# A hybrid encoder layer on one core: the shared sums queued later, two small product groups on column halves, the last norm's parameters loaded later

## The chip, the cores and the metric

The kernel runs on one core of a Trainium2 chip. The core has TensorE (PE, matrix products into PSUM), VectorE (DVE), ScalarE (ACT), GpSimd (POOL) and SyncE (SP), whose queue issues most DMAs here. Each engine runs its own instructions in order, and semaphores tie them together. The metric is the device time of one execution in microseconds (us); lower is better.

## The reference, cut to what matters

One layer of width 1024 over 1024 tokens, with 16 learned tokens put in front and dropped at the end, all in float32. The stream is projected once; three mixers read the projection (HGRN2 heads, Mamba-2 heads, S5 channel groups); their outputs are concatenated and projected, and a squared-ReLU MLP of width 4096 follows.

```python
proj = h @ w_in[l]
q_a, f_a, i_a, g_a, z_b, xbc_b, dt_b, u_c = jnp.split(proj, split_idx, axis=-1)
y_a = hgrn2_mixer(q_a, f_a, i_a, g_a, ...)   # 6 heads, chunks, a decay per channel
y_b = mamba2_mixer(z_b, xbc_b, dt_b, ...)    # 6 heads, chunked state space
y_c = s5_mixer(u_c, ...)                     # diagonal complex recurrence
mixed = jnp.concatenate([y_a, y_b, y_c], axis=-1) @ w_out[l]
h = layer_norm(ALPHA * h + mixed, ln1_g[l], ln1_b[l])
ff = jnp.square(jax.nn.relu(h @ w_mlp_in[l])) @ w_mlp_out[l]
h = layer_norm(ALPHA * h + ff, ln2_g[l], ln2_b[l])
```

In the HGRN2 mixer, a chunk's output is what the state before it gives, plus the products of q and k within the chunk, each pair of tokens weighted by the decay between them.

## The kernel before

**Precision.** A large product is made of float32 halves: `split` (L98) casts a tile to a high part on ScalarE (L100) and subtracts it on VectorE for the low part (L87), and `mm3` (L107) adds three products, high by high, high by low and low by high (L108 to L110).

**Weights.** `load_raw` (L182) issues on SP the DMA of a 128x512 half tile into one of a ring of four raw buffers; the split puts it into one of eight pairs of high and low tiles. A load therefore waits until the split of four loads before is done, and a split until the products are done that last read its pair. In the last phase a second ring of four joins.

**Order of the work.** The program is written as lists of small steps (units), and `run` (L1578) merges several lists in proportion. The framework then builds each engine's own instruction order from this program order as priority, by its own estimate of when things are ready, and fixes it: on the chip an engine never passes an instruction that waits. What order two instructions of one engine get can be forced with an ordering edge between them.

**The mixers.** HGRN2 works on 8 chunks of 128 tokens, 4 in each half of the sequence. Within a chunk, `hg_level` (L777) goes through seven levels h = 1, 2, 4 to 64: at each, products of the running `A` (decayed q) and `B` (decayed k) give the scores between the neighbouring blocks of length h. At levels up to 32 there is one product for each of three channel tiles and each half of the tokens (L791), the halves going to PSUM partitions 0 to 63 and 64 to 127, that is to the array's two column halves. The last level (L783) has one product a channel tile for both heads of it, with its output on partitions 0 to 63 alone, and ScalarE copies it to `Py` (L785). `hg_out` (L805) first forms the sums of q times k per token (L810): `QK` as weights with all 128 columns, against a constant with two columns, for each channel tile; then the other products of the chunk's output in 64-column halves (L814 to L817).

**Output projection.** `wout_units` (L1091) makes, for four token tiles t of a half and two column halves dh, a unit of 24 matmuls and one accumulation into `acc[t]` on VectorE (`accumulate`, L1079). The first unit of a dh loads the eight w_out half tiles, for dh = 0 also the eight mixed tiles. PSUM for it comes from a ring of two (`p_o`).

**MLP.** The 4096 hidden columns are done in 8 pieces of 4 tiles of 128. Pieces 0 to 3 run plainly over the first half of the tokens, piece 0 then over the second half (`p0`: four upward units "u", one weight fetch "w", eight downward units "d"). Pieces 4 to 7 run over both halves with a seven-product Strassen scheme upward (`up_strassen`, L1290) and downward (`strassen_units`, L1390 on). Pieces 1 and 2 over the second half form one more Strassen block, the double piece, and piece 3 over the second half ends the kernel.

**Shared sums.** The four Strassen pieces share sums of the normed input, made once by `row_sums` (L1246): `fetch3` and `third` subtract two halves of the first tokens' rows (they need only the first half of the tokens), `first`, `second` and `fourth` need the second half too. All but `second` write their split result to DRAM (`away`, T_d), from where `stream(n)` (L1239) brings sum n into the tiles of the first half's input, four DMAs of 512 KB, before each piece that needs it. In a piece, `w5` loads four w_mi half tiles, adds two pairs (`tw`) on VectorE and splits them for the first product, on sum 1.

**Where the change touches.** The eight units of `fetch3` and `third` are merged with the eight units of the second half's output projection; the sums with p0 by a string of letters ("s" is `stream(1)`); `load_gb(2)` puts scale and shift of the last norm (broadcast to 128 partitions) on SP just ahead of the double piece; `finish(t)` norms and stores the first half's tokens and is merged with the double piece's 32 units.

```python
run(wout_units(1, (6, 7, 0, 1, 2, 3, 4, 5), True), sums[0])
...
for c in "u u f u w f u f f d d s n d n d n d n d d d".split():
    (p0 if c in "udw" else sums[1]).pop(0)()
...
gb = gbp.tile([128, 2, D], F32, tag="gb", name="gb2")
load_gb(2)
...
run(us, [lambda t=t: finish(t) for t in h0])
```

Of the kernel before, what the change touches and what calls it, by code (L numbers as in the profile page):

```python
# [11 lines left out]
ALU = mybir.AluOpType  # L12
# [8 lines left out]
NPRE = 4  # L21
# [3 lines left out]
ALPHA = 2.0 ** 0.25  # L25
# [41 lines left out]
def tile_trunk(ctx, tc, xT, x_tok, w_vdt, w_ch, w_out, w_mi, w_mo, glu_w, pack, kconst,  # L67
# [15 lines left out]
    def add(e, out, a, b):  # L83
        e.tensor_tensor(out=out, in0=a, in1=b, op=ALU.add)  # L84

# [3 lines left out]
    def stt(out, a, s, b, op0, op1):  # L89
        V.scalar_tensor_tensor(out=out, in0=a, scalar=s, in1=b, op0=op0, op1=op1)  # L90

# [90 lines left out]
    def load_raw(src):  # L182
        rings.append(rings.pop(0))
        raw = rings[-1]()
        nc.sync.dma_start(out=raw, in_=src)
        return raw

    def load_h(src, dst=None):
# [588 lines left out]
    def hg_level(c, h):  # L777
        hb = HB[c % len(HB)]
        ps = p_sc()
        if h == 64:  # L780

            for ct in range(3):
                PE.matmul(ps[0:64, ct * 128:ct * 128 + 128].rearrange("p (g l) -> p g l", g=2),  # L783
                          hb["B"][:, ct, 0:64], hb["A"][:, ct, :, 64:128], start=True, stop=True, skip_group_check=True)
            S.copy(hb["Py"][0:64], ps[0:64, 0:384].rearrange("p (h l) -> p h l", h=6))  # L785
        else:

            for ct in range(3):
                for x in range(2):
                    Av = hb["A"][:, ct, :, hms[x]].rearrange("p g (b two l) -> p g b two l", two=2, l=h)[:, :, :, 1, :]  # L790
                    PE.matmul(ps[hms[x], ct * 64:ct * 64 + 64].rearrange("p (g b l) -> p g b l", g=2, l=h),  # L791
                              hb["B"][:, ct, hms[x]], Av, start=True, stop=True, skip_group_check=True)
            src = ps[:, 0:192].rearrange("p (h b l) -> p h b l", h=6, l=h)
            dst = hb["P"].rearrange("p h (b two l) -> p h b two l", two=2, l=h)[:, :, :, 1, :]
            if h == 32:

                S.copy(hb["Py"][64:128], hb["P"][64:128])
                S.copy(dst[0:32, :, 0], src[0:32, :, 0])
                S.copy(hb["Py"][64:96, :, 32:64], src[64:96, :, 0])
            else:  # L800
                m = km2[:, h.bit_length() - 1].unsqueeze(1).to_broadcast([128, 6, 32])
                V.copy_predicated(dst, m.rearrange("p h (b l) -> p h b l", l=h), src)
        hg_decay(hb, h, 128, True)

    def hg_out(c):  # L805
# [3 lines left out]
        for ct in range(3):  # L809
            PE.matmul(po[:, 384 + 2 * ct:386 + 2 * ct], hb["QK"][:, ct], ind2, start=(ct == 0), stop=False,  # L810
                      skip_group_check=True)
        for h in range(6):
# [261 lines left out]
    def mix_in(half, k):  # L1074
        src_d, o = ((mixA_d, 0), (mixB_d, 3), (mixC_d, 6))[k // 3]
        raw = load_raw(src_d[:, k - o, HALF * half:HALF * half + HALF])
        split(hk(half, 0, POS[k]), hk(half, 1, POS[k]), raw)

    def accumulate(t, dh, lhs, w, first, c0=0, nc_=512):  # L1079

# [5 lines left out]
        if first:  # L1086
            stt(acc[t][:, cs], acc[t][:, cs], ALPHA, ps, ALU.mult, ALU.add)
        else:
            add(V, acc[t][:, cs], acc[t][:, cs], ps)

# [155 lines left out]
    def row_sums(t2h, t2l, pool):  # L1246
# [38 lines left out]
        def units(f):  # L1285
            return [lambda k=k: f(k) for k in range(4)]

        return units(fetch3) + units(third), units(first) + [lambda: stream(1)] + units(second), units(fourth)

    def up_strassen(js, A, t2, again, ahead, beside):  # L1290

# [86 lines left out]

        us += [w5] + go("c", "s1", "1", True, keep(1, 0)) + [lambda: stream(3)] + beside[:2]
        us += [w1] + go("a", "11", "11", True, keep(0, 1)) + beside[2:]  # L1380
# [8 lines left out]

    def strassen_units(fs, ts_, keep, b_op, sums=None, again=False, beside=()):  # L1390

# [162 lines left out]
        if sums is not None:  # L1554
            us += up_strassen(js, A, sums, again, ahead, list(beside))
        else:
# [110 lines left out]
    sums = row_sums(t2h, t2l, ff2)  # L1667
    run(wout_units(1, (6, 7, 0, 1, 2, 3, 4, 5), True), sums[0])
    run(sum([[lambda t=t: norm1(t), lambda t=t: h1_transpose(t)] for t in h1_], []), pre[cut:])
# [3 lines left out]
    p0 = piece(0, [1], (), HALF, True)  # L1673
    for c in "u u f u w f u f f d d s n d n d n d n d d d".split():
        (p0 if c in "udw" else sums[1]).pop(0)()
    for p in range(NPRE, NP):
        js = list(range(NF * p, NF * p + NF))
        for f in strassen_units((js[:2], js[2:]), (list(h0), list(h1_)), True, lambda name: [None] * 2, (t2h, t2l), p < NP - 1,
                                sums[2] if p == NPRE else ()):
            f()  # L1680
    gb = gbp.tile([128, 2, D], F32, tag="gb", name="gb2")
    load_gb(2)
    rings_t2 = lambda: arp.tile([128, 512], F32, tag="t2h", name="raw", bufs=4)
# [5 lines left out]
                        lambda name: [[x[:, j] for x in b4] for j in range(4)] if name in ("b1", "b3", "b7") else [None] * 4)  # L1689
    run(us, [lambda t=t: finish(t) for t in h0])  # L1690
    rings[:] = [f for f in rings if f is not rings_t2]
# [99 lines left out]
```

## Time and profile before

| | |
|---|---|
| median of 3 runs | 1224.56 us (1223.6 to 1226.91) |
| the profiled execution's own time | 1227.8 us |
| its span, first to last instruction | 1225.7 us |
| mean granted TensorE clock | 0.994 of full speed |
| busy: PE, DVE, ACT, POOL | 1194.5, 898.6, 596.0, 24.5 us |
| DMA | 180.97 MB, mean 148 GB/s |

Times in the views count from the span's start. A row of a timeline has the start, the duration, engine, line, operation, the tiles (written <- read), the partitions x elements, a count, and in brackets how long the engine had stood idle before it and what ended that. A row of the view of waits has who waited <- for whom: microseconds in total, times, the longest. A row of the windows view has the stretch, its length, the busy time of the engine with the number of instructions that touch the stretch, the granted clock of TensorE, the busy share of the DMA engines and their GB/s. A row of a group has busy time, mean ns of one, and the idle time before. SPq is SP's queue issuing DMAs; PE records are two for each float32 product that is not split, one for each of a split one.

### The profile page before, as it was taken

The numbers are of one execution on the slowest core, as the hardware profiler recorded it, in microseconds if no ns is written. First come the engines' busy times: TensorE is split into PE (matmuls) and PEld (weight loads), VectorE is DVE, ScalarE is ACT, GpSimd is POOL, SyncE is SP. The second block draws the span as 40 slices with busy tenths as digits, with TensorE's granted clock in tenths as the row PEclk, the third lists the DMA queues.
The fourth block names the chain that finished last, engine by engine and source line by source line (L and its number), as shares of the span: only waits on it lengthen the run. The fifth ranks groups of instructions, "written<-read, shape, count | busy, mean of one in ns | idle before, by whom it ended". The sixth has DMA issues, their size and how long they took to land.

```text
span 1225.7 us, 19167 instructions
## 1 busy us (share of the span) xinstructions
PE 1194.5 (97%) x6932; PEld 984.8 (80%) x6932; DVE 898.6 (73%) x1953; ACT 596.0 (49%) x1312; POOL 24.5 (2%) x35
## 2 busy tenths in 40 slices
PE   8999999999999999999998998999999999999997
PEld 8988788778787888887886886878878778788886
DVE  7824866787777797757564776779597796899956
ACT  5343233544775376545453354463553635546542
POOL 0000000000000000000000000000000000003003
PEclk9999999999999999999998999999999999999999
DMA  8142343224557252323159367863635627357331
GB/s 272 55 148 86 78 122 114 104 85 131 164 187 233 65 151 81 100 79 113 52 170 324 100 180 235 266 198 103 237 106 188 224 71 252 124 160 243 121 112 68
DMA packets 111693, 180.97 MB, mean 148 GB/s; under 512 B 10992, under 2 KB 45424, under 8 KB 111600
## 3 DMA queue, kind: packets, MB, share of 16 engines
q1 hardware_dynamic: 108144, 173.47, 44.5%
q10 hardware_dynamic: 3456, 6.29, 1.3%
q8 instruction: 54, 0.88, 0.3%
q14 instruction: 39, 0.32, 0.1%
HBM read 148.43 MB, written 30.24 MB: 146 GB/s over the span
## 4 chain that ended last, share of the span: by engine, by line
PE 70%; DMA 13%; DVE 11%; ACT 3%; issue 2%; SPq 1%; ACTq 0%; POOL 0%; POOLq 0%; DVEq 0%
PE pg L108 11%; PE pg L109 11%; PE pg L110 11%; PE pm_o L108 7%; PE pm_o L109 7%; PE pm_o L110 7%; DMA raw<-w_mi 4%; PE pm_sc L109 2%; PE pm_sc L110 2%; PE pm_sc L108 2%; PE pm_sc L791 2%; DMA raw<-w_out 2%; DVE lo L87 1%; DMA xr<-xT 1%; DMA raw<-w_mo 1%
## 5 line engine op out<-in xcount | busy, mean ns | idle before, releaser
L87 DVE TENSOR_TENSOR lo<-raw,hi 128x512 fp32r<-128x512 f32 x260 | 177.1, 692 | 120.4 <-ACT hi L100 117.3
L100 ACT CAST hi<-raw 128x512 fp32r<-128x512 f32 x260 | 159.1, 619 | 181.7 <-PE pg L109 79.5
L108 PE MATMUL pm_o<-hi,fh 128*128 128x512 f32 x232 | 94.0, 405 | 3.6 <-DVE acc L90 3.3
L110 PE MATMUL pm_o<-hi,fl 128*128 128x512 f32 x232 | 91.6, 395 | 0.0
L109 PE MATMUL pm_o<-lo,fh 128*128 128x512 f32 x232 | 91.6, 395 | 0.0
L108 PE MATMUL pg<-x0h,hi 128*128 128x264 f32 (+1 forms) x264 | 85.3, 323 | 0.4 <-ACT uch L640 0.4
L108 PE MATMUL pg<-h1a,hi 128*128 128x512 f32 (+1 forms) x224 | 82.7, 370 | 2.2 <-ACT hi L100 1.4
L110 PE MATMUL pg<-x0h,lo 128*128 128x264 f32 (+1 forms) x264 | 84.5, 320 | 0.1
L109 PE MATMUL pg<-x0l,hi 128*128 128x264 f32 (+1 forms) x264 | 83.9, 318 | 0.0
L109 PE MATMUL pg<-h1a,hi 128*128 128x512 f32 (+1 forms) x224 | 81.2, 363 | 0.7 <-DMA h1a<-T_d 0.7
L110 PE MATMUL pg<-h1a,lo 128*128 128x512 f32 (+1 forms) x224 | 81.4, 364 | 0.0
L110 PE MATMUL pg<-h1b,lo 128*128 128x512 f32 x176 | 68.6, 390 | 0.1
L108 PE MATMUL pg<-h1b,hi 128*128 128x512 f32 x176 | 68.5, 389 | 0.0
L109 PE MATMUL pg<-h1b,hi 128*128 128x512 f32 x176 | 68.5, 389 | 0.0
L109 PE MATMUL pg<-x1l,hi 128*128 128x512 f32 x168 | 66.4, 395 | 0.0
L110 PE MATMUL pg<-x1h,lo 128*128 128x512 f32 x168 | 66.3, 395 | 0.0
L108 PE MATMUL pg<-x1h,hi 128*128 128x512 f32 x168 | 66.2, 394 | 0.0
L84 DVE TENSOR_TENSOR acc<-acc,pm_o 128x512 f32<-128x512 f32 (+1 forms) x77 | 52.0, 675 | 18.6 <-PE pm_o L110 17.6
L100 ACT CAST fh<-ar 128x512 fp32r<-128x512 f32 (+1 forms) x72 | 39.5, 560 | 40.5 <-DVE ar L87 32.0
L100 ACT CAST hi<-tw 128x512 fp32r<-128x512 f32 x52 | 31.9, 620 | 51.4 <-DVE tw L87 28.9
L108 PEld LDWEIGHTS pm_o<-hi,fh 128*128 128x128 f32 x232 | 44.1, 190 | 13.4 <-DVE acc L90 3.8
L108 PEld LDWEIGHTS pg<-x0h,hi 128*128 128x128 f32 x264 | 49.6, 188 | 5.2 <-ACT uch L640 0.8
(459 smaller groups left out, 3042.7 us busy)
## 6 DMA issues: line engine op xcount, KB each, us to landing
raw<-w_mo SPq DMA_DIRECT2D x140, 256.0 KB, 3.4
raw<-w_mi SPq DMA_DIRECT2D x112, 256.0 KB, 3.3
h1a<-T_d SPq DMA_DIRECT2D x48, 512.0 KB, 6.4
raw<-w_ch SPq DMA_DIRECT2D x48, 256.0 KB, 3.3
raw<-w_out SPq DMA_DIRECT2D x32, 256.0 KB, 3.8
acc<-x_tok SPq DMA_DIRECT2D x8, 512.0 KB, 5.5
b_d<-sig SPq DMA_DIRECT2D x16, 256.0 KB, 3.0
ar<-b_d SPq DMA_DIRECT2D x16, 256.0 KB, 5.3
```

Source lines behind the costliest of these rows:

```text
L84: e.tensor_tensor(out=out, in0=a, in1=b, op=ALU.add)
L87: e.tensor_tensor(out=out, in0=a, in1=b, op=ALU.subtract)
L100: S.copy(hi, src)
L108: PE.matmul(out, wh, xh, start=start, stop=False, **kw)
L109: PE.matmul(out, wh, xl, start=False, stop=False, **kw)
L110: PE.matmul(out, wl, xh, start=False, stop=stop, **kw)
L791: PE.matmul(ps[hms[x], ct * 64:ct * 64 + 64].rearrange("p (g b l) -> p g b l", g=2, l=h), hb["B"][:, ct, hms[x]], Av, start=True, stop=Tru ...
```

## The change

- The units `fetch3` are now traced after the first five units of the second half's output projection, and their fetches get an ordering edge on SP behind the last w_out load so far (`fetched`). Each `third` gets an edge on VectorE behind the accumulation two before the last one traced (`behind`).
- The last level's product is split by head, one to each column half, 64 moving columns each, and the copy to `Py` becomes two. The sums of q times k are split into the two halves of the tokens, with 64 columns of weights each.
- `stream(1)` is taken out of p0's string; in the first Strassen piece it comes after `w5`, and `w5`'s VectorE instructions get an edge behind the fourth accumulation from the end, the fifth of p0's eight.
- `load_gb(2)` becomes a unit (`last_gb`) merged with the double piece, ahead of the four `finish`, with an edge on SP behind the last load traced before it. With five units merged into 32, it is traced after the seventh, and the `finish` units after the 13th, 20th, 26th and 32nd instead of the 8th, 16th, 24th and 32nd.

```diff
     def load_raw(src):
         rings.append(rings.pop(0))
         raw = rings[-1]()
-        nc.sync.dma_start(out=raw, in_=src)
+        fetched[0] = nc.sync.dma_start(out=raw, in_=src)
         return raw
...
             for ct in range(3):
-                PE.matmul(ps[0:64, ct * 128:ct * 128 + 128].rearrange("p (g l) -> p g l", g=2),
-                          hb["B"][:, ct, 0:64], hb["A"][:, ct, :, 64:128], start=True, stop=True, skip_group_check=True)
-            S.copy(hb["Py"][0:64], ps[0:64, 0:384].rearrange("p (h l) -> p h l", h=6))
+                for g in range(2):
+                    PE.matmul(ps[hms[g], ct * 64:ct * 64 + 64], hb["B"][:, ct, 0:64], hb["A"][:, ct, g, 64:128],
+                              start=True, stop=True, skip_group_check=True)
+            Pg = hb["Py"].rearrange("p (c g) l -> p c g l", g=2)
+            for g in range(2):
+                S.copy(Pg[0:64, :, g], ps[hms[g], 0:192].rearrange("p (c l) -> p c l", c=3))
...
         for ct in range(3):
-            PE.matmul(po[:, 384 + 2 * ct:386 + 2 * ct], hb["QK"][:, ct], ind2, start=(ct == 0), stop=False,
-                      skip_group_check=True)
+            for x in hms:
+                PE.matmul(po[x, 384 + 2 * ct:386 + 2 * ct], hb["QK"][:, ct, x], ind2, start=(ct == 0), stop=False,
+                          skip_group_check=True)
...
+    sums_done = []
+
+    def behind(f, n):
+
+        with tc.issue_after(sums_done[-1 - n].ins):
+            f()
+
     def accumulate(t, dh, lhs, w, first, c0=0, nc_=512):
...
         if first:
-            stt(acc[t][:, cs], acc[t][:, cs], ALPHA, ps, ALU.mult, ALU.add)
+            sums_done.append(stt(acc[t][:, cs], acc[t][:, cs], ALPHA, ps, ALU.mult, ALU.add))
         else:
-            add(V, acc[t][:, cs], acc[t][:, cs], ps)
+            sums_done.append(add(V, acc[t][:, cs], acc[t][:, cs], ps))
...
-        return units(fetch3) + units(third), units(first) + [lambda: stream(1)] + units(second), units(fourth)
+        return units(fetch3) + units(third), units(first) + units(second), units(fourth)
...
-        us += [w5] + go("c", "s1", "1", True, keep(1, 0)) + [lambda: stream(3)] + beside[:2]
+        if first:
+            us += [lambda: behind(w5, 3), lambda: stream(1)]
+        else:
+            us.append(w5)
+        us += go("c", "s1", "1", True, keep(1, 0)) + [lambda: stream(3)] + beside[:2]
...
-    run(wout_units(1, (6, 7, 0, 1, 2, 3, 4, 5), True), sums[0])
+
+    wu = wout_units(1, (6, 7, 0, 1, 2, 3, 4, 5), True)
+    for f in wu[:5]:
+        f()
+    for f in sums[0][:4]:
+        with tc.issue_after(fetched[0].ins):
+            f()
+    for i in range(4):
+        if wu[5 + i:]:
+            wu[5 + i]()
+        behind(sums[0][4 + i], 2)
...
-    for c in "u u f u w f u f f d d s n d n d n d n d d d".split():
+    for c in "u u f u w f u f f d d n d n d n d n d d d".split():
         (p0 if c in "udw" else sums[1]).pop(0)()
...
-    load_gb(2)
+
+    def last_gb():
+
+        with tc.issue_after(fetched[0].ins):
+            load_gb(2)
+
...
-    run(us, [lambda t=t: finish(t) for t in h0])
+    run(us, [last_gb] + [lambda t=t: finish(t) for t in h0])
```

`tc.issue_after(i)` adds the edge to those instructions of its block that run on `i`'s own engine; the block's instructions on other engines get none.

More of the change, by code (lines that the diff above doesn't have):

```diff
@@ L83, in add @@
     def add(e, out, a, b):
-        e.tensor_tensor(out=out, in0=a, in1=b, op=ALU.add)
+        return e.tensor_tensor(out=out, in0=a, in1=b, op=ALU.add)
     def sub(e, out, a, b):
@@ L89, in stt @@
     def stt(out, a, s, b, op0, op1):
-        V.scalar_tensor_tensor(out=out, in0=a, scalar=s, in1=b, op0=op0, op1=op1)
+        return V.scalar_tensor_tensor(out=out, in0=a, scalar=s, in1=b, op0=op0, op1=op1)
     def ts(e, out, a, s1, s2=None, op0=ALU.mult, op1=None):
@@ L184, in load_raw @@
         raw = rings[-1]()
-        nc.sync.dma_start(out=raw, in_=src)
+        fetched[0] = nc.sync.dma_start(out=raw, in_=src)
         return raw
+    fetched = [None]
     def load_h(src, dst=None):
@@ L1286, in units, with up_strassen @@
             return [lambda k=k: f(k) for k in range(4)]
-        return units(fetch3) + units(third), units(first) + [lambda: stream(1)] + units(second), units(fourth)
-    def up_strassen(js, A, t2, again, ahead, beside):
+        return units(fetch3) + units(third), units(first) + units(second), units(fourth)
+    def up_strassen(js, A, t2, first, again, ahead, beside):
         us = []
@@ L1388, in up_strassen, with strassen_units @@
         return us
-    def strassen_units(fs, ts_, keep, b_op, sums=None, again=False, beside=()):
+    def strassen_units(fs, ts_, keep, b_op, sums=None, first=False, again=False, beside=()):
         us = []
@@ L1554, in strassen_units @@
         if sums is not None:
-            us += up_strassen(js, A, sums, again, ahead, list(beside))
+            us += up_strassen(js, A, sums, first, again, ahead, list(beside))
         else:
@@ L1677, in tile_trunk @@
         js = list(range(NF * p, NF * p + NF))
-        for f in strassen_units((js[:2], js[2:]), (list(h0), list(h1_)), True, lambda name: [None] * 2, (t2h, t2l), p < NP - 1,
+        for f in strassen_units((js[:2], js[2:]), (list(h0), list(h1_)), True, lambda name: [None] * 2, (t2h, t2l), p == NPRE, p < NP - 1,
                                 sums[2] if p == NPRE else ()):
```

## The prediction

> **What bounds the kernel now.** The page comes first: which engine fills the span.
>
> ```profile
> span 1225.7 us, 19167 instructions
> PE 1194.5 (97%) x6932; PEld 984.8 (80%) x6932; DVE 898.6 (73%) x1953; ACT 596.0 (49%) x1312; POOL 24.5 (2%) x35
> ```
>
> TensorE is busy 1194.5 of 1225.7 us. What is to be gained is therefore of two kinds: the 31 us in which it stands still, and matmuls that cost fewer of its own microseconds. The view of waits, for PE alone, says who ended its longest pauses (total, times, longest).
>
> ```profile
> PE pm_o L109 <- DVE lo L87: 4.7, 2, 4.1
> PE pm_o L108 <- DVE acc L90: 3.3, 1, 3.3
> PE pg L108 <- ACT hi L100: 1.4, 2, 1.1
> PE pg L109 <- DMA h1a<-T_d: 0.7, 1, 0.7
> PE pg L108 <- DMA h1a<-T_d: 0.7, 1, 0.7
> ```
>
> Two pauses are of over 3 us, and the diff has an edit beside each of these lines. So next the timelines of PE, DVE and SP's queue around the first one.
>
> ```profile
> 656.77 0.50 PE L108 MATMUL pm_o<-hi,h1b 128*128 128x512 f32 x1
> 661.42 0.80 PE L109 MATMUL pm_o<-lo,h1b 128*128 128x512 f32 x1 [4.15 <-DVE lo L87]
> ...
> 660.07 0.69 DVE L87 TENSOR_TENSOR ar<-ar 128x512 f32<-128x512 f32 x1 [4.61 <-DMA ar<-b_d]
> 660.68 0.68 DVE L87 TENSOR_TENSOR lo<-raw,hi 128x512 fp32r<-128x512 f32 x1
> ...
> 652.08 1.83 SPq L1257 DMA_DIRECT2D ar<-b_d  x2
> 656.09 0.84 SPq L1257 DMA_DIRECT2D ar<-b_d  x2
> ...
> 656.10 0.62 ACT L100 CAST hi<-raw 128x512 fp32r<-128x512 f32 x1 [1.11 <-DMA raw<-w_out]
> ```
>
> The reader is to see an order on VectorE, not a lack of speed. TensorE needs the low part of the last w_out half tile (`lo`). The split that makes it stands on VectorE behind a subtraction of the shared sums (`third`), and that one waits 4.61 us for its operand, whose fetch SP issued only at 652 to 656. The windows view shows what follows a pause.
>
> ```profile
> 646.70:656.70 10.00, 10.00 (x46) 1.00 0.93 296
> 661.42:667.57 6.15, 6.15 (x15) 0.50 0.97 317
> 762.76:766.74 3.98, 3.98 (x10) 0.57 0.39 132
> ```
>
> The column after the count is the granted clock: 1.00 before, 0.50 after the pause. 15 matmuls took 6.15 us where at 46 in 10.00 us they would take 3.3, so 2.9 us more went. After the second pause 10 matmuls took 3.98 instead of 2.2 us: 1.8 us more.
>
> **The change part by part.** Terms are against the profiled execution's own 1227.8 us (its span is 1225.7); the median of the runs is 1224.56, 3.2 us lower, and I take that off at the end.
>
> **A, the shared sums.** The eight fetches now stand in SP's queue behind the last w_out half tile, and the four `third` steps on VectorE behind the fourth, fifth and sixth accumulation. Nothing is left between the low part at 660.68 and its cast. Gone are the pause of 4.15 and the slow stretch of 2.9: 7.1 us. What is late next is the w_out half itself: TensorE reached it at 656.77, when its high part had just been cast (656.10 and 0.62), and the low part takes 0.68 more, so I leave 0.4 us of pause: 6.7 gained. Where the sums go, w_out's second halves are loading.
>
> ```profile
> 678.05 2.37 SPq L185 DMA_DIRECT2D raw<-w_out  x4
> ...
> 670.55 0.69 DVE L90 SCALAR_TENSOR_TENSOR acc<-acc,pm_o 128x512 f32<-128x512 f32 x1 [5.20 <-PE pm_o L110]
> ```
>
> VectorE idles 5.20 us per accumulation there, and a `third` needs two subtractions of 0.69, so the work itself is covered. The four late w_out halves are not roomy, which makes a rival below. Queued behind the moved fetches on SP are the next w_mo and w_mi loads; those are fetched ahead of their use.
>
> **B, the first `w5`.**
>
> ```profile
> 762.76 0.50 PE L108 MATMUL pm_o<-hi,fh 128*128 128x512 f32 x1 [3.33 <-DVE acc L90]
> ...
> 761.42 0.69 DVE L84 TENSOR_TENSOR tw<-raw 128x512 f32<-128x512 f32 x1 [5.18 <-DMA raw<-w_mi]
> 762.03 0.68 DVE L90 SCALAR_TENSOR_TENSOR acc<-acc,pm_o 128x512 f32<-128x512 f32 x1
> ...
> 754.34 0.87 SPq L1244 DMA_DIRECT2D h1a<-T_d  x2
> 755.27 7.67 SPq L185 DMA_DIRECT2D raw<-w_mi  x4
> ```
>
> The same pattern: the sum `tw` of the first Strassen piece waits 5.18 us on VectorE for w_mi, and an accumulation that frees a PSUM bank waits behind it. The w_mi loads were late because `stream(1)` stood ahead of them on SP. The change sets `w5`'s VectorE work behind the fifth of eight accumulations and `stream(1)` behind the loads. Gained: 3.33 and 1.8, 5.1 us. `w5` then has three downward products to finish in, 36 matmuls or some 8 us at the rate above, and needs two adds, two casts and two subtractions, some 3 us: covered. But TensorE now comes to this piece 5 us sooner, while its weight loads go through four raw buffers, whose pace is that of DMA.
>
> ```profile
> 775.88 6.64 SPq L185 DMA_DIRECT2D raw<-w_mi  x4
> 784.54 1.85 SPq L1244 DMA_DIRECT2D h1a<-T_d  x4
> ...
> 802.03 2.15 SPq L1244 DMA_DIRECT2D h1a<-T_d  x4
> ```
>
> The streams at 784.54 and 802.03 stand behind such loads, and the second one already gave the pauses of 0.7 and 0.7. If nothing of this queue moves, all 5.1 come back; if it moves with TensorE, nothing does, and if the earlier first stream also helps the later ones, those 1.4 go too. Part of it follows TensorE, since splits wait for tiles that products free, so I charge 1.5 us.
>
> **C, scale and shift of the last norm.**
>
> ```profile
> 1047.40 0.50 PE L108 MATMUL pg<-h1a,hi 128*128 128x512 f32 x1 [1.13 <-ACT hi L100]
> ...
> 1033.84 0.42 SPq L1137 DMA_DIRECT2D gb<-ln_gb  x1
> 1036.58 2.23 SPq L185 DMA_DIRECT2D raw<-w_mi  x2
> ```
>
> One of the two broadcasts is issued ahead of the w_mi loads on which this pause of 1.13 hangs. Moved behind the double piece's fetches it frees them: 1.1 us. In exchange the four norms of the first half come later on an engine that has no room to spare:
>
> ```profile
> 1150.00:1160.00 10.00, 9.99 (x20) 1.00 0.34 109
> ...
> L1112 DVE BATCH_NORM_STATS2 bst<-acc 128x6 f32<-128x512 f32 x8 | 5.2, 665 | 0.0
> L90 DVE SCALAR_TENSOR_TENSOR acc<-acc,mv,gb 128x768 f32<-128x768 f32 x4 | 4.2, 1053 | 0.0
> L90 DVE SCALAR_TENSOR_TENSOR acc<-acc,lrs,gb 128x768 f32<-128x768 f32 x4 | 4.0, 1008 | 0.0
> ```
>
> Only 8.2 us of these norms read gb, and TensorE never waits in that stretch, so I charge nothing; the rival has the other end.
>
> **D, column halves.** Windows of PE that run from a group's first matmul to the start of the next group, and one of mixed half-column matmuls.
>
> ```profile
> 246.42:246.92 0.50, 0.50 (x14) 1.00 0.00 0
> 253.40:254.20 0.80, 0.80 (x8) 1.00 0.57 190
> 612.53:613.19 0.66, 0.66 (x8) 1.00 0.00 0
> 255.26:256.55 1.29, 1.29 (x50) 1.00 0.00 0
> L785 ACT COPY Py<-pm_sc x8: 472/473/477, 254.3 to 609.5; 64x384 f32<-64x384 f32 x8
> ```
>
> The last level now costs 0.80 us a chunk (6 records on one column half); the other levels do the same volume in 12 records on both halves in 0.50. Eight chunks by 0.30: 2.4 us. The sums of q times k take 0.66 (6 full-width records of two columns). As 12 half-width ones at the pace of the fourth row (50 in 1.29, or 0.026 each) they take 0.31, a gain of 0.35 a chunk, or 2.8 in all; at the first row's 0.50 it is 1.3. I take 2.0. No row shows half-width weights with two moving columns, so zero gain is the lower bound; twice the instructions on the same full-width pace would lose 5.3, and the fourth row, where each record has weights of its own, excludes that. The copy of 0.473 becomes two shorter ones on ScalarE, busy 49%: nothing, or at most some 0.2 a chunk if the next product waited for it.
>
> The fourth row is also where a rule of the Trainium skill is to be weighed. "TensorE: Matmul & The Clock Gate", Part 3, says that a weight load overlaps running matmuls only when its row group differs, and column halves share their rows; with its load time of columns over 1.2 GHz, halving the columns and doubling the loads would gain nothing, and the total would be 2.0 us higher. This trace disagrees: 0.026 us per record is less than the 0.053 that the page's formula gives for 64 columns.
>
> **Sum.** 6.7 + 5.1 − 1.5 + 1.1 + 2.4 + 2.0 = 15.8; 1227.8 − 15.8 = 1212.0 on the profiled execution's scale, less 3.2: 1208.8 us.
>
> **The rivals.** *The first Strassen piece gives its gain back.* For it: the two streams above, and a queue that does not reorder. Against it: `stream(1)` no longer blocks the loads, so the queue starts sooner. Price: the rest of B, 3.6, to 1212.4, and up to 1.8 more for a halved clock: about 1214.
>
> *The sums still come in between.* The new order binds one engine each: `third` may start right after the fourth accumulation, just when w_out's last four half tiles (issued at 678.05) are to be split. If a subtraction that waits for its fetch is put ahead of one of those splits, the pause moves to the fifth accumulation. Price: half of A to all of it, 3.4 to 6.7: 1212.2 to 1215.5. This is also the way in which the change would not do what it says.
>
> *Half-width q times k gains nothing.* Then D has 2.4 alone: 1210.8.
>
> *Slower: the norms fall into the full stretch.* If gb lands so late that VectorE has nothing else to do until then, the norms' 5.2 + 4.2 + 4.0 = 13.4 us fall behind the products' splits and accumulations between 1140 and 1170, and TensorE waits for them, with 2.9 us of half clock after each of two pauses: 19.2 us, so 1228.0. It decides from the point at which VectorE, waiting for gb before 1130, idles longer than it is ahead of TensorE; how far ahead that is no row tells, only that the view of waits lists no long pause there. Against it: there are other splits to fill the time with, and the norms need gb for 8.2 of the 13.4 only.
>
> **How the numbers follow.** Forecast 0.62; the first piece gives back 0.17; sums in between 0.10; q times k gains nothing 0.07; slower by the norms 0.04. The lower end: A with 7.1, B with 5.1 and 1.4 of the later stream, C 1.1, D 2.4 + 2.8 make 19.9, so 1204.7; 1204. The upper end takes the rivals up to 1215.5 and 1.5 for a build order that shifts elsewhere: 1217. About 0.3%, or 3.7 us, is what a measurement tells from no change: all cases but the last lie beyond it, and I leave 0.03 for several rivals together: faster 0.93, same 0.03, slower 0.04.
>
> **What would show it.** In the changed kernel PE's waits have no line of 4.1 us on `lo` and none of 3.3 on `acc`; the granted clock is 1.00 after the first output projection unit of the second half; the last level and q times k have twice their matmul records, a group of the first takes 0.50 and one of the second about 0.4; gb is issued after the double piece's first w_mi loads and 1.13 is gone. The first rival shows as PE waits on `h1a<-T_d` of over 3 us in the first Strassen piece, the second as a wait on `lo` at the fifth accumulation, the slower one as waits on `acc` or `fl` near 1140 to 1170. I am wrong if TensorE's pauses sum to more than 20 us.

## The result, and the profile after

The changed kernel took 1217.68 us in the median of six runs (1214.67 to 1220.67), the kernel before 1226.56 in as many beside it (1223.6 to 1228.36): a ratio of the means of 0.9932, 95% interval 0.9914 to 0.9950, or 8.3 us less (6.1 to 10.5). Timed once more in another job, the ratio was 0.9917 (0.9898 to 0.9937), 10.2 us less. The direction was forecast; the size was to be 15.8, to 1208.8 us, and 1217.7 lies just above the forecast's upper end of 1217.

The page of the changed kernel, its first two lines of numbers:

```profile
span 1212.6 us, 19370 instructions
PE 1186.5 (98%) x7028; PEld 976.8 (81%) x7028; DVE 898.2 (74%) x1953; ACT 596.3 (49%) x1320; POOL 24.7 (2%) x35
```

The 96 added matmuls are there, and TensorE is busy 8.0 us less; it stands still for 26.1 us instead of 31.2. The span is 13.1 us shorter, more than the runs are apart, so this pair of executions flatters the change. The profiled execution of the changed kernel (1214.67 us) was the fastest of its six runs, and the one of the kernel before (1227.8) was above its median. The view of waits for PE, between 640 and 830 us, answers to the two long pauses:

```profile
PE pg L108 <- ACT ar L1383: 2.0, 1, 2.0
PE pm_o L108 <- DVE acc L90: 0.8, 1, 0.8
PE pm_o L109 <- DVE lo L87: 0.2, 1, 0.2
```

The pauses of 4.15 on `lo` and 3.33 on `acc` are gone. The first line is new: a product waits for ScalarE's copy of a sum (L1383). The windows view, PE alone: the last level, q times k (both, as in the prediction, from a group's first matmul to the start of the next group), the second output projection, and the stretch after the new pause.

```profile
605.04:605.54 0.50, 0.50 (x14) 1.00 0.00 0
608.80:609.17 0.37, 0.37 (x13) 1.00 0.00 0
646.00:656.00 10.00, 10.00 (x46) 1.00 0.44 138
781.64:787.00 5.36, 5.36 (x16) 0.68 0.33 114
```

The last level takes 0.50 us a chunk as forecast and the sums of q times k 0.37 (0.66 before; about 0.4 forecast). After the new pause the granted clock is 0.68. Where that pause is made, the timelines of SP's queue, ScalarE and PE show:

```profile
765.99 1.54 SPq L185 DMA_DIRECT2D raw<-w_mi  x2
767.58 3.70 SPq L1257 DMA_DIRECT2D h1a<-T_d  x4
772.83 2.13 SPq L185 DMA_DIRECT2D raw<-w_mi  x2
...
774.26 0.59 ACT L1383 COPY ar<-pg 128x512 f32<-128x512 f32 x1
780.48 0.62 ACT L100 CAST hi<-raw 128x512 fp32r<-128x512 f32 x1 [5.63 <-DMA raw<-w_mi]
781.00 0.58 ACT L1383 COPY ar<-pg 128x512 f32<-128x512 f32 x1
...
781.64 0.50 PE L108 MATMUL pg<-h1a,hi 128*128 128x512 f32 x1 [1.97 <-ACT ar L1383]
```

Read it from the bottom. The fourth product of the first Strassen piece adds to a bank whose content must first be copied out. The copy stands on ScalarE behind a cast that waits 5.63 us for w_mi, and that load, issued at 772.83, landed 7.6 us later, behind the four stream fetches of 512 KB each.

To see where gains come and go, take stretches of each profiled execution: from the first matmul of the second output projection to p0 (the sums' pause lies there), from p0 to the first Strassen piece (the pause of `w5`), from the first to the seventh product of that piece, and from its first product to the end of its seventh and last. Starts are those of PE's timeline; all in us. The runs named are told in the next section.

| kernel | projection to p0 | p0 to the piece | first to seventh product | whole piece |
|---|---|---|---|---|
| before | 76.33 | 49.76 | 32.64 | 39.97 |
| before, profiled again | 76.24 | 49.27 | 32.64 | 39.35 |
| changed | 71.37 | 43.83 | 36.56 | 41.99 |
| changed, profiled again | 71.89 | 43.77 | 36.34 | 42.19 |
| sums alone | 71.69 | 48.81 | 32.64 | 38.64 |
| `w5` alone | 74.95 | 43.55 | 36.67 | 42.49 |
| gb alone | 71.25 | 49.89 | 32.66 | 38.86 |
| halves alone | 70.71 | 51.05 | 32.89 | 40.56 |
| sums and `w5` | 71.73 | 43.72 | 38.73 | 45.83 |
| sums and `w5`, no fourth stores | 70.59 | 43.91 | 35.16 | 41.03 |
| changed, no fourth stores | 73.30 | 44.74 | 33.30 | 39.15 |
| changed, fourth sums later | 71.64 | 44.12 | 37.83 | 43.77 |
| changed, weights ahead of sums | 69.74 | 44.61 | 35.42 | 41.27 |
| all but `w5` | 72.24 | 51.06 | 32.64 | 39.01 |

The second and the last column are steady. Over all twenty profiles the second stretch is 43.5 to 45.5 us where `w5` is moved and 48.8 to 51.5 where it is not. The whole piece takes 38.1 to 40.6 us without the move, and 41.2 to 45.8 with it where the stores are made as before. The third column overstates the loss: a part of it comes back in the seventh product, where the kernel before has its two pauses of 0.7 us. The first column is not steady: gb alone and the halves alone keep the old order of the sums, and their stretches are no longer than the changed kernel's.

### The profile page after: what moved, and what is told of

Same layout as the page of the kernel before. It is cut to its first block, busy times and chain, and to the rows that moved or that the text cites. A ratio compares the mean times of both kernels' runs of the same rounds, so it can differ in the third digit from the quotient of the medians.

```text
span 1212.6 us, 19370 instructions
## 1 busy us (share of the span) xinstructions
PE 1186.5 (98%) x7028; PEld 976.8 (81%) x7028; DVE 898.2 (74%) x1953; ACT 596.3 (49%) x1320; POOL 24.7 (2%) x35
## 4 chain that ended last, share of the span: by engine, by line
PE 72%; DVE 12%; DMA 10%; ACT 3%; issue 2%; SPq 0%; POOL 0%; POOLq 0%; DVEq 0%; ACTq 0%
PE pg L108 12%; PE pg L109 12%; PE pg L110 12%; PE pm_o L108 6%; PE pm_o L110 6%; PE pm_o L109 6%; DMA raw<-w_mi 4%; PE pm_sc L109 2%; PE pm_sc L110 2%; PE pm_sc L108 2%; PE pm_sc L796 2%; DVE lo L87 2%; DMA xr<-xT 1%; ACT hi L100 1%; DVE ctg L81 1%
## 5 line engine op out<-in xcount | busy, mean ns | idle before, releaser
L110 PEld LDWEIGHTS pg<-x0h,lo 128*128 128x128 f32 x264 | 49.7, 188 | 3.8 <-issue 0.6
```

The lines of the kernel that those rows point to most:

```text
L110: PE.matmul(out, wl, xh, start=False, stop=stop, **kw)
```

## The experiments

**Theory 1**: the four parts do what the diff says, and part of what they gain is lost again in the first Strassen piece, whose transfers cannot be had sooner, and at the weights behind the moved sums. **Rivals**: the parts never gained that much and the profile of before was of a slow execution; or the new waits come from the order on ScalarE, not from the transfers.

**Each part alone.** The edit of each is its own part of the diff put into the kernel before: the sums' units, `w5` and `stream(1)`, `last_gb`, the two groups of half-width matmuls.

```diff
+    for f in sums[0][:4]:
+        with tc.issue_after(fetched[0].ins):
+            f()
...
+        behind(sums[0][4 + i], 2)
```
```diff
+            us += [lambda: behind(w5, 3), lambda: stream(1)]
```
```diff
+    run(us, [last_gb] + [lambda t=t: finish(t) for t in h0])
```
```diff
+                for g in range(2):
+                    PE.matmul(ps[hms[g], ct * 64:ct * 64 + 64], hb["B"][:, ct, 0:64], hb["A"][:, ct, g, 64:128],
...
+            for x in hms:
+                PE.matmul(po[x, 384 + 2 * ct:386 + 2 * ct], hb["QK"][:, ct, x], ind2, start=(ct == 0), stop=False,
```

> Part A alone (fetches and third steps of the shared sums queued later; all else as before). Theory 1, the terms were sized right and new waits give part back: the 4.15 us pause on the low part of w_out and the half-clock stretch behind it go (-7.1), and the w_mo loads of piece 3, now queued on SP behind the eight fetches of first and second, come late and cost 2.3 at the first transposes: about -4.9 us, ratio 0.996. Theory 2, the sums merely move between w_out's last four splits: -3.4 to 0, with a PE wait on lo at the fifth accumulation.

> Part B alone (w5's VectorE work behind the fifth accumulation, stream 1 behind its loads; all else as before). Theory 1: 5 to 6 us less up to the first product of the first Strassen piece, then 3 to 4 us back in that piece, where TensorE waits for a PSUM bank whose copy on ScalarE stands behind a cast of late w_mi: about -2 us, ratio 0.998. Theory 2, the piece follows TensorE as forecast: -3.6 us, ratio 0.997.

> Part C alone (scale and shift of the last norm loaded within the double piece). Theory 1: the 1.13 us pause ahead of the last Strassen piece's fourth product shrinks by about 0.6, and the double piece pays 1 to 2 us for norms that come later: 0 to +1 us, ratio 1.000 to 1.001. Theory 2, as forecast: -1.1 us, ratio 0.999.

> Part D alone (last level and q times k on column halves). Theory 1: 0.30 us a chunk from the level and 0.15 to 0.25 from q times k, eight chunks, half of it before the first output projection and half before the second: -3.9 us, ratio 0.997. Theory 2, the weight loads on halves do not overlap: q times k gains nothing, -2.4 us, ratio 0.998.

Measured: sums 0.9961 (0.9948 to 0.9975), -4.8 us; `w5` 0.9981 (0.9965 to 0.9998), -2.3 us; gb 1.0007 (0.9992 to 1.0021), +0.9 and not to be told from nothing; halves 0.9958 (0.9945 to 0.9971), -5.2 us. The forecast had -6.7, -3.6, -1.1 and -4.4. Added up, -11.4, of which each term is known to some 1.5 to 2 us.

**Of the halves, q times k alone**, with the last level as before:

> Of the column halves the sums of q times k alone; the last level, the sums, the first product's weights and the norm's scale and shift as before. Forecast's step: -2.0 us, 0.9983. The rival of the record (both halves in the same rows, so that their weight loads gain nothing): 0 to -0.3 us, 1.000. Theory 1 (the profile's rows: twelve half-width matmuls take about 0.5 us where six full ones took 0.66): -1.5 to -2.5 us.

0.9981 (0.9968 to 0.9994), -2.3 us: half-width weights do gain, and the rival of the record falls. The interval (0.7 to 3.9 us) does not settle the size; by the rows, 0.66 less 0.37 over eight chunks is 2.3, and 1.5 if one counts from the start of the product ahead of the group to the next group (0.88 before, 0.69 after).

**Sums and `w5` together**, and the kernel before once more:

> The sums queued later and the first Strassen product's weights behind the third accumulation, without the halves and without the later load. If the two add up as they were alone: -4.8 and -2.3, -7.1 us, 0.9942. Theory 1 (with both pauses gone the weights, the sums and the streamed rows are wanted sooner than the transfers can land them, and the two share one gain): -4 to -6 us, 0.995 to 0.997. The forecast had -10.3.

(`w5` stands behind the fifth of p0's accumulations here too, not behind the third.)

> The kernel before, timed and profiled as the others are. Both theories: a ratio of 1.000. Theory 1 (the parts gain 13 us in like executions, and the waits that come back leave 9): its profiled execution has the same two long pauses near 661 and 765 us and its stages stand within 1.5 us of the first profile. Theory 2 (the first profile of the kernel before was of a slow execution, and part of the 13.1 us between the two profiles is chance): its span is 2 to 4 us below the first one's 1225.7, and its pauses are shorter at the same places.

The two together: 0.9974 (0.9959 to 0.9988), -3.2 us, less than the sums bring alone. The view of waits for PE from 640 to 830 us in this run:

```profile
PE pg L108 <- ACT hi L100: 3.0, 1, 3.0
PE pg L108 <- ACT ar L1379: 2.6, 1, 2.6
PE pm_o L108 <- DVE acc L90: 0.8, 1, 0.8
```

Two pauses of together 5.6 us stand inside the Strassen piece, at its fourth and seventh product; the table has 38.73 us there instead of 32.64. The kernel before, again, came out at 1.0003 (0.9988 to 1.0019), its span at 1226.8, and the first three stretches of the table within 0.5 us of the first profile. So the two long pauses of that profile were no accident, and that rival falls; what flatters the first pair most is the changed kernel's execution, the fastest of its six.

How long the two pauses are is another matter. In the eight profiles without `w5`'s edit, the one on `acc` is 2.7 to 4.9 us. In the seven that keep the old order of the sums, the one on `lo` is 1.5 to 5.3 us; it is 2.00 in gb alone and 1.53 in the halves alone, and no half clock follows there. Windows of PE, six us from the end of the pause, in these two:

```profile
660.99:666.99 6.00, 6.00 (x26) 1.00 1.03 374
653.24:659.24 6.00, 6.00 (x26) 1.00 1.04 362
```

**The changed kernel again, and its two new waits taken on one by one.** The first edit below puts the weights ahead of the sums (`mark` is the last load traced when the first of these fetches is due), the second the copies ahead of the casts of `w2` (`kept` is the last copy of a sum so far).

```diff
+        mark[0] = mark[0] or fetched[0].ins
+        with tc.issue_after(mark[0]):
+            sums[1].pop(0)()
```
```diff
+        def after_kept(f):
+            with tc.issue_after(kept[0].ins):
+                f()
...
-        us += [w2] + go("b", "12", "21", True, total(0, 1))
+        us += [(lambda: after_kept(w2)) if first else w2] + go("b", "12", "21", True, total(0, 1))
```

> The changed kernel unchanged, timed in the same job as the next three, and profiled once more. Theory 1 (the four parts gain 13 to 14 us together, and two new waits give 4 to 6 back: the first hidden-layer product waits for its weights behind eight fetches of the sums, the first Strassen piece waits for ScalarE copies that stand behind a cast): the ratio is again near 0.993, about -8 us, and the profile shows both waits again: pauses of together 0.8 to 2.5 us within 15 us of the first up product, and one of 1.5 to 3 us about 20 us after the Strassen piece begins, with matmuls at half rate behind it. Theory 2 (the profile of the kernel before was taken in a slow execution, and the parts never gained more than 9 us; the waits are accidents of one execution): at least one of the two waits is missing here and the time does not change for it.

> The changed kernel, with the fetches of the second half's first and second sums queued behind the last weights that were asked for before them. Theory 1: the first hidden-layer product of the first piece no longer waits for its low weights; the 2.3 us that the stretch lost come back, 0.998 of the changed kernel, about -10 us against the kernel before. Rival: the sums that come later make the first Strassen products wait instead, and nothing is gained (0.993 against the kernel before).

> The changed kernel, with the casts of the second Strassen product's weights queued on ScalarE behind the four copies of the first product's sums instead of ahead of them. Theory 1: the pause of 1.97 us for a bank of PSUM and the half-rate matmuls behind it (together 3.9 us) go, and some of it comes back where those casts are now later: -2 to -4 us against the changed kernel. Rival (the raw tiles' fetches, not the order on ScalarE, limit the first Strassen piece): the pause moves to the cast's own matmul and nothing is gained.

> The changed kernel with both edits of the two runs before. Theory 1: the gains add up, -4 to -6 us against the changed kernel, about 0.989 against the kernel before. Rival: 0.993, as the changed kernel.

(The texts name the products wrongly: the weights that wait near 692 us are those of a downward product of a plain piece, and `w2`'s are for the Strassen piece's fifth product, while the copies are those of its third.) Measured, in the order of the texts: 0.9917 (0.9898 to 0.9937), 0.9916 (0.9894 to 0.9938), 0.9903 (0.9885 to 0.9922), 0.9897 (0.9876 to 0.9918). Both waits are there in the repetition, so they are no accident. With the sums' fetches moved, the first stretch is 69.74 us instead of 71.4 to 71.9 and the wait on `lo` is gone, but the time is the same. With the copies moved, the pause at the fourth product shrinks from 2.0 and 2.2 to 0.9 us, and one of 1.2 stands at the seventh, where the changed kernel had none in its first profile and 1.1 in its second. Neither edit brought the 2 to 4 us expected; both together have 1.8 us against the changed kernel in the same job, within the intervals. So the order on ScalarE is a part at most: what stood behind one late transfer next waited for another. That reading is argued from the profiles; the times do not tell these kernels apart.

**The transfers, directly.** One kernel makes the fourth sums of the first Strassen piece (four fetches, eight stores) later in the piece, and one leaves the eight stores out.

```diff
-        us += [w1] + go("a", "11", "11", True, keep(0, 1)) + beside[2:]
+        us += [w6] + go("a", "s2", "2", False, keep(0, 0)) + beside[:2]
+        us += [w7] + go("a", "s3", "3", False, total(1, 0)) + (beside[2:] or [lambda: stream(4)])
```
```diff
+                nc.sync.dma_start(out=strm[n][j][i].bitcast(F32), in_=T_d[n if n != 4 else 3][:, j, 2 * i:2 * i + 2])
...
-            for j in range(2):
+            for j in range(2 if n != 4 else 0):
                 S.dma_start(out=T_d[n][:, j, k], in_=o[j].bitcast(F32))
```

> The changed kernel with the fourth sums of the first Strassen piece (four fetches, eight stores) made beside its third and fourth products instead of beside its first and second, and their stream fetched one product later. Theory 1 (the first piece loses 3.9 us because more is to be moved between 755 and 785 us than the transfers land; the stores are a part of it): the pause of about 2 us near 782 us shrinks below 1 us, and the kernel is 1 to 4 us faster than the changed one. Rival (the order on ScalarE): the pause stays, 0 us. Second rival (the bytes only move to the next product): a pause of 1 to 3 us between 795 and 830 us, 0 to -1 us.

> The changed kernel without the eight stores of the fourth sums (2 MB); the last product of each Strassen piece reads the third sums in their place, so what it computes is another product of the same size. Theory 1 (bytes): the pause near 782 us is under 0.8 us, and -2 to -4 us against the changed kernel. Rival (order on ScalarE): the pause stays between 1.5 and 2.2 us and the time is the changed kernel's.

Later: 0.9905 (0.9885 to 0.9924), and the second rival of that text is what the profile shows: the pause at the fourth product is 1.0 us, that at the seventh 2.3, and the seventh begins 37.83 us after the first (six matmuls of the next step stand ahead of it there, some 1.4 us). The bytes were only moved. Without the stores: 0.9909 (0.9894 to 0.9925). Windows view of this kernel, all engines, around the place of the pause (PE, PEld, DVE, ACT, POOL, then clock, DMA share, GB/s):

```profile
755.00:770.00 15.00, 15.00 (x68) 12.43 (x67) 12.13 (x20) 6.20 (x11) 0.00 (x0) 1.00 0.44 140
770.00:785.00 15.00, 15.00 (x67) 12.21 (x66) 8.55 (x14) 7.23 (x14) 0.00 (x0) 1.00 0.75 252
```

The same windows of the changed kernel:

```profile
755.00:770.00 15.00, 15.00 (x68) 12.40 (x67) 13.12 (x22) 6.44 (x11) 0.00 (x0) 1.00 0.65 215
770.00:785.00 15.00, 13.03 (x54) 10.35 (x53) 6.90 (x12) 6.57 (x13) 0.00 (x0) 0.93 0.76 280
```

Without the stores the DMA engines move 140 GB/s instead of 215 in the first window, and TensorE has no pause in the second. ScalarE's timeline has the same copy behind the same cast:

```profile
779.97 0.62 ACT L100 CAST hi<-raw 128x512 fp32r<-128x512 f32 x1 [3.49 <-DMA raw<-w_mi]
780.50 0.58 ACT L1383 COPY ar<-pg 128x512 f32<-128x512 f32 x1
```

The load that the cast waits for is issued at 772.85 and has landed at 779.97, only 0.5 us sooner than in the changed kernel (772.83 and 780.48). The rest of the pause of 1.97 us is missing because TensorE comes to the piece 1.6 us later (764.82 instead of 763.18), the two stretches before it having taken 73.30 and 44.74 instead of 71.37 and 43.83. So this run alone does not show that the stores make the pause. What the stores do to the loads stands in the waits of SP's queue in the changed kernel, 760 to 785 us:

```profile
SPq L185 <- DMA T_d<-fl: 1.4, 1, 1.4
SPq L1257 <- DMA T_d<-fh: 1.1, 1, 1.1
```

The queue stands still until a store has landed, once ahead of a stream fetch and once ahead of a w_mi load. Both rows are missing without the stores. Why a fetch waits for a store, no run here shows. In the time this kernel is 1 to 2.5 us below the changed one, within the intervals.

**All but `w5`, and the two edits without the stores.**

> The changed kernel with the first Strassen product's weights and stream where the kernel before has them: the sums, the halves and the norm's load alone. Forecast's step: 5.1 less 1.5, so this kernel is 3.6 us slower than the changed one, 0.9960 against the kernel before. Theory 1 (what the weights' edit gains before the piece is given back within it): 0 to 2 us slower than the changed one, 0.992 to 0.9945.

> The sums and the first product's weights as in the run of the two together, without the eight stores of the fourth sums (the last product of each Strassen piece reads the third sums in their place, a product of the same size). Theory 1 (the transfers of the first piece are why the two gained 3.2 and not 7.1): no pause over 1.5 us between 785 and 815 us, -6 to -9 us against the kernel before, 0.9927 to 0.995. Rival (the two share a gain for another reason): -3 to -4 us, 0.997.

> The kernel before without the same eight stores, the last product of each Strassen piece on the third sums. Theory 1 (its pause of 3.3 us ahead of the piece lets the transfers get ahead, so that the stores cost it little): 0 to -1 us, 0.999 to 1.000. Rival (the stores cost every kernel the same): -3 us or more, under 0.9975.

Without `w5`'s edit the changed kernel has 0.9944 (0.9924 to 0.9965), 6.9 us less than before: next to the other three the edit is worth 1.5 to 3.3 us by the two timings of the changed kernel. That is about what it brings alone (2.3), and the intervals do not exclude the 3.6 forecast. Sums and `w5` without the stores: 0.9954 (0.9938 to 0.9970), -5.6 us, where they had -3.2 with them; the kernel before without the stores: 1.0022 (1.0001 to 1.0043), +2.7 us, where 0 to -1 was expected. Leaving the stores out does not speed up the kernel before, then, and the two edits are 0.9932 against it (0.9954 over 1.0022, some 8 us, of which the two intervals leave 5 to 11): about the 7.1 that they bring one by one. That comparison rests on the 2.7 us by which the kernel before is slower without the stores, and why it is slower is open; its profile has the same two long pauses. The waits for PE from 640 to 830 us, of the two edits without the stores:

```profile
PE pg L108 <- ACT ar L1379: 1.1, 1, 1.1
PE pg L108 <- ACT hi L100: 0.9, 1, 0.9
PE pm_o L108 <- DVE acc L90: 0.6, 1, 0.6
```

The same two lines as with the stores, 2.0 us instead of 5.6. The w_mi load behind the first of them is issued 7.6 us after the piece's first product instead of 9.3, and takes no less time to land (8.8 us instead of 8.6). So the stores delay that load mainly by its issue, as in the two rows of SP's queue above (here, with the stores, 2.7 and 0.6 us).

**A version that goes further.** The weights and the copies ahead, and gb loaded as before; then the fourth sums later as well.

> The changed kernel with the weights fetched ahead of the sums, the copies ahead of the casts, and the last norm's scale and shift loaded where the kernel before loads them. Theory 1 (the later load costs 0.9 us, as the run of that part alone had it): about 11.5 to 13 us faster than the kernel before, 0.990 to 0.9895. Rival (the 0.9 was noise): as the run with both edits, 0.9897.

> The changed kernel with the weights fetched ahead of the sums, the copies ahead of the casts, the last norm's scale and shift loaded as before, and the fourth sums later. Theory 1: 1 to 3 us below the version without the last edit (0.9889), 0.9865 to 0.988. Rival: as that version.

0.9889 (0.9863 to 0.9915) and 0.9905 (0.9889 to 0.9922). With the 0.9897 of both edits alone, the medians of these three are 1211.95 to 1214.65 us; the fourth sums later alone had 1214.15. All overlap with the changed kernel's 0.9917 and 0.9932, so a gain of a few us over it is likely, not shown; the last edit shows none.

## Why the prediction was right in direction and wrong in size

**A failed in size.** Of the 6.7 us, the run alone measured 4.8 (3.1 to 6.4). The pause and its half clock are gone, as said. Two steps failed. The first is "Gone are the pause of 4.15 and the slow stretch of 2.9: 7.1 us", which takes the price from one execution. In the seven profiles with the old order the pause is 1.5 to 5.3 us, the half clock behind it is missing in two of them, and the stretch to p0 takes 70.7 to 76.3 us, so the profile of before stood near the upper end. The second step, argued from the profiles and not seen in the times, is "those are fetched ahead of their use", of the loads queued behind the moved fetches. In the changed kernel SP's queue reads:

```profile
682.31 5.82 SPq L1270 DMA_DIRECT2D ar<-b_d  x8
692.42 2.29 SPq L185 DMA_DIRECT2D raw<-w_mo  x4
```

and around them TensorE waits on `lo` (0.23) and `acc` (0.80), with starts stretched beside it. Where the eight fetches are put behind the w_mo loads, the stretch takes 69.74 (69.58, 71.21 and 69.48 in the three other kernels that have the edit); in the nine other profiles with the sums' edit it takes 70.6 to 73.3. By which step the fetches delay the weights is not settled: the first cast there waits not for its load but for a tile that a product still reads.

**B failed at its charge.** The 5.1 us before the piece came, and more: the stretch is 5.9 us shorter. "I charge 1.5 us" for the first Strassen piece is the step that failed. To the start of its seventh product the piece gave back 3.9 in the first pair of profiles and 3.7 in the second. Of this 1.9 and 0.9 came back in the seventh product, so that the whole piece is 2.0 and 2.8 us longer. With `w5` alone it is 2.5 us longer than in the first profile of before, and with the sums too 5.9. In the times the two edits together gain 3.2 where they gain 7.1 one by one; but in the run of all but `w5` the same edit is worth as much next to the sums as alone, so that loss stands in one run only.

That was the first rival, put at 0.17, come half true. Its place was right and its sign only nearly: not a wait on `h1a<-T_d` itself, but on a copy behind a cast behind a load behind those fetches. The argument against it, that splits wait for tiles which products free, looked at what TensorE sets. By the table, the pause of 3.33 us had been a time in which the transfers got ahead: wherever it goes while the stores stay, the piece behind it grows. The stores of the fourth sums lie in the same 25 us, and the prediction did not count them.

**C failed.** The forecast gave it 1.1 us; alone it measured +0.9 (-1.0 to +2.6). The step that failed is "it frees them: 1.1 us". The pause at the last product before the double piece, on which it rests, is no property of gb's place. It was 1.13 in the first profile of before; in the second one, and in the version with both edits and gb as before (PE's timeline, one row each):

```profile
1047.29 0.50 PE L108 MATMUL pg<-h1a,hi 128*128 128x512 f32 x1 [1.77 <-ACT hi L100]
```

```profile
1037.63 0.50 PE L108 MATMUL pg<-h1a,hi 128*128 128x512 f32 x1 [1.90 <-ACT hi L100]
```

Over all profiles it runs from 0.2 to 3.3 us with gb loaded as before, and from 0.5 to 1.3 with gb later. In exchange each of the nine with gb later has a pause of 0.4 us on `fh` some 15 us behind it, which none of the others has:

```profile
PE pg L109 <- DVE lo L87: 0.4, 1, 0.4
PE pg L108 <- ACT fh L100: 0.4, 1, 0.4
```

(The view of waits of the changed kernel from 1035 us on; `fh` is the second row.)

**D held.** 4.4 forecast, 5.2 measured (3.6 to 6.7). The last level is 0.30 us a chunk shorter as worked out; q times k is 0.29 shorter where 0.25 was taken, and 0.19 counted from the start of the product ahead of it. All chunks are done before the second output projection, and that begins at 646.4 to 649.6 us in the eleven profiles with both groups halved, at 651.3 to 654.6 in the eight with neither: some 5 us. The rule of "TensorE: Matmul & The Clock Gate", Part 3, in the Trainium skill, by which, with that page's load time, column halves would have gained nothing in q times k, is contradicted by the run of that part alone.

**The scale.** The median of before, 1224.56 from three runs, was 1225.5 to 1226.9 in later jobs. The changed kernel's ratio on 1224.56 would be 1216.2 us; some 1.5 of the distance between 1208.8 and 1217.7 is this. The other 7.5 (15.8 less 8.3) are, by the runs of the parts alone, 1.9 from A, 1.3 from B and 2.0 from C less 0.8 from D, 4.4 together; the 3.1 left over are about what A and B lose when both are made (7.1 alone, 3.2 together). By the second timing of the changed kernel, 10.2 us less, only 1.2 are left over, so this remainder lies within the noise.

The prediction's sign of being wrong, pauses of more than 20 us in all, decides nothing. TensorE stands still for 26.1 us, but of the 31.2 before, the forecast's own terms take away only 4.15, 3.33 and 1.13 less 0.4, so 23.0 would have been left had all of it come true.

Of the other rivals, the sums did not come in between (no wait on `lo` at the fifth accumulation), and the norms did not fall into the full stretch: gb landed at 1088.79 and 1090.08, the first norm read it at 1089.48, and TensorE waited for none of them.

## What to carry to other kernels

A pause on the busiest engine can also be a time in which the transfers get ahead. Before booking its removal, count what has to be moved in the next 20 to 40 us, stores and streams included, by the GB/s that the windows show, and ask which load then lands last. Parts that gain one by one in front of the same queue must be tried together, since together they may gain less. And a pause is to be priced from several executions: its length and the half clock behind it differed by several us between kernels that run the same order.

## What the runs showed of the hardware

How long the half clock lasts after a pause is not set by the pause. Windows of PE from the end of a pause of 2.59 and one of 3.04 us in the run of sums and `w5`:

```profile
789.08:794.00 4.92, 4.92 (x22) 1.00 0.32 106
808.74:813.00 4.26, 4.26 (x12) 0.62 0.42 127
```

The first cost no clock at all, and in the changed kernel a pause of 1.97 us gave 0.68. The half clock has lengths of its own. Windows of PE in the kernel before, cut where the granted clock changes:

```profile
660.78:667.61 6.83, 6.19 (x15) 0.50 0.96 319
763.18:766.59 3.41, 3.41 (x10) 0.50 0.44 150
```

The first begins 0.64 us before its pause ends. Between the first and the last 11 us of all twenty profiles, every stretch of half clock is 3.41 or 6.83 us long. The Trainium skill, "TensorE: Matmul & The Clock Gate", Part 1, says that the clock falls after an idle window of about 3.4 us, that this window runs freely and that the count of slow matmuls varies from run to run. The variation and the length of the window agree with these rows; a pause of well under 3.4 us (1.97, and 1.77 in the second profile of before) was enough for a slow stretch here.

DMA engines moved 323 GB/s at a busy share of 0.89 between 770 and 785 us where the fourth sums were made later, against 280 at 0.76 in the changed kernel: the rate at which the changed kernel's loads were late was not the most that the engines can move.
